# Attention with an additive bias: the second half of pair 0's q is loaded behind the first half of the bias

## The chip, the cores and the metric

The kernel runs on one core of a Trainium2 chip. The time is the device time of one execution in microseconds (us); the median of five executions stands for the kernel. The engines of the core are PE (matrix products), ACT (activation functions, here exponentials), DVE (vector work), POOL (GpSimd, which here issues most of the loads) and SP (which issues the stores and a few early loads). "Landing" is the moment at which a load's data is in on-chip memory and its semaphore is complete.

## The reference

Four batches of eight heads, 1024 positions, head size 64, all in float32; one bias matrix of 1024 by 1024 is shared by all heads.

```python
scores = scale * np.matmul(q, k.transpose(0, 1, 3, 2))      # scale = 1/8
scores = scores + bias
scores_max = np.max(scores, axis=-1, keepdims=True)
attn = np.exp(scores - scores_max) / (np.sum(np.exp(scores - scores_max), axis=-1, keepdims=True) + 1e-8)
return np.matmul(attn, v)
```

The kernel leaves the maximum out and uses exp(s + b) = exp(s) exp(b): the exponential of the bias is made once, and each head's exponentials are multiplied by it.

## The kernel before

**Tiling.** The 32 heads form 16 pairs. A pair's k and q are transposed on PE, so that the head's 64 dimensions of both heads fill the 128 rows. A *bank* is one product of 128 key positions with 512 query positions of one head: `banks` lists 512 of them, by pair, query half `qh`, key block `kc` and head. For pair 0, banks 0 to 15 have qh = 0, in the order of kc with the two heads beside each other, and banks 16 to 31 have qh = 1. A *slot* is one ACT instruction: slot 0 has bank 0, slot 1 has banks 1 and 2, and from slot 2 on each has three (slot 2: 3, 4, 5; slot 5: 12, 13, 14; slot 6: 15, 16, 17). S0, S1, ... are the slots here.

**The work of a slot.** `s_fill` has PE write the scores of a slot into one of two buffers (line 130). `s_exp` has ACT write the exponentials (line 137). `mul_pair` has DVE multiply them by the exponential of the bias (lines 156, 159, 162). `av_bank` has PE multiply them with v, which carries a column of ones for the denominators (line 187), and at the end of a head and half DVE divides (lines 197, 199) and SP stores.

**The bias.** It is loaded in two halves of 512 query rows, `btraw[:, :QC, :]` and `btraw[:, QC:, :]`, in 16 bits, 1 MB each. `b_fill(qh, k0)` transposes four key blocks of one half on PE into one of the same two score buffers (line 145), and `b_exp` takes the exponential (line 150). There are four such steps, called B(0,0), B(0,4), B(1,0) and B(1,4) here.

**The start.** Pair 0's first half of q and k comes by SP and ACT in float32 and is converted on the chip. The second half of k (`kr0`, line 261) and of q (`qr0`, line 262) and the first bias half (line 263) are issued by POOL one after the other on its one queue, and then v, the second bias half, and the loads of pairs 1 and 2. Slots 0 to 2 are written out by hand. Bank 8 is the first that reads the second half of k, bank 16 the first that reads the second half of q.

**The order of the rest.** From slot 3 on, a planner in the kernel's own text emits the instructions. It keeps three clocks (`t_act`, `t_pe`, `t_dve`), adds an assumed cost for each step, and takes in turn what can start first. What it emits is a fixed order for each engine: an instruction that waits holds back all behind it on its engine. The sequence of slots and bias steps is fixed by `order`: S3, S4, S5, S6, B(0,0), S7, B(0,4), S8, S9, B(1,0), S10, B(1,4), S11 and so on. Between these fills the planner puts the *pieces* (transpositions of half a k or half a q, `transpose_pe`, line 89, with the copy on DVE at line 98 for q and line 102 for k) and the products with v. A piece is placed no earlier than its data is assumed to land:

```python
bias_at = [13300, 20800]                                                 # line 338: the two bias halves, ns
raw_at = {0: (5900, 7800), 1: (22200, 23500), 2: (26000, 28500)}         # line 339: (k, q) of pairs 0, 1, 2
```

The times count in ns from the start of the span. These values steer the order alone; the waits themselves are made by semaphores, whatever the values are. The piece (0, 0, 1) is the second half of pair 0's q. When it has been copied, `run` issues the loads of pair 3 and of pair 2's v.

**The end.** The last eight banks of the last head (NB-8 to NB-1) are multiplied with v by `av_last` in two halves of 256 query rows (x = 0, 1), line 223. `pe_last` chooses which banks come next.

Of the kernel before, what the change touches and what calls it, by code (L numbers as in the profile page):

```python
# [15 lines left out]
def kernel(  # L16
# [15 lines left out]
    nc = tc.nc  # L32
# [7 lines left out]
    QC = NCH // 2  # L40
# [5 lines left out]
    bf_ = bias.rearrange("a b (p c) k -> p (a b c) k", p=P)  # L46
# [12 lines left out]
    btraw = consts.tile([P, NCH, S], BF)  # L59
# [47 lines left out]
    NB = len(banks)  # L107
# [106 lines left out]
    def av_last(x, bs, tag):  # L214
        first = len(last_left[x]) == 8
        if first:
            po[x] = (ps_x if tag != "s" else ps_s).tile([P, M, D1], F32, tag=tag, name="po")
        acc = po[x]
        for b in bs:
            last_left[x].remove(b)  # L220
        for i in range(M):
            for b in bs:
                nc.tensor.matmul(acc[:, i, :], e_at(b, 1)[:, 0, (x * M + i) * P:(x * M + i + 1) * P],
                                 vall[:, 2 * NP - 1, banks[b][3], :], start=first and i == 0 and b == bs[0],
                                 stop=not last_left[x] and b == bs[-1], skip_group_check=True)
        if last_left[x]:
            return None

        def evac():
            oh = small.tile([P, M, D], F32, name=f"oh{x}")  # L230
            rs = small.tile([P, M, 1], F32, name=f"rh{x}")
            nc.vector.reciprocal(rs[:], acc[:, :, D:D1])
            q = (nc.scalar, nc.sync)[x]
            if x == 0:
                for i in range(M):
                    nc.scalar.activation(oh[:, i, :], acc[:, i, :D], ACTF.Copy, scale=rs[:, i, :])
            else:
                nc.vector.tensor_tensor(oh[:], acc[:, :, :D], rs[:].to_broadcast([P, M, D]), op=ALU.mult)
            q.dma_start(out=of[2 * NP - 1][:, QC + x * M:QC + (x + 1) * M, :], in_=oh[:])
        return evac  # L240

    with tc.manual_schedule():
# [16 lines left out]
        nc.gpsimd.memset(qT0[D:, 0, :HQ], 0.0)  # L259
        nc.gpsimd.memset(qT0[:D, 1, :HQ], 0.0)  # L260
        nc.gpsimd.dma_start(out=kr0[:, :, QC:, :].rearrange("p t c d -> p t (c d)"), in_=kf[0][:, :, QC * D:])  # L261
        nc.gpsimd.dma_start(out=qr0[:, :, QC:, :].rearrange("p t c d -> p t (c d)"), in_=qf[0][:, :, QC * D:])
        nc.gpsimd.dma_start(out=btraw[:, :QC, :], in_=bf_[:, :QC, :])
        for x in range(2):
            for y in range(2):
                nc.vector.memset(mask[x * D:(x + 1) * D, y, :], 1.0 if x == y else 0.0)
# [68 lines left out]
        act_end = []  # L335
        x_free = {"xa": T0 - 500, "xb": T0 + 100}
        x_unit = {}
        bias_at = [13300, 20800]
        raw_at = {0: (5900, 7800), 1: (22200, 23500), 2: (26000, 28500)}
        pieces = [(0, 0, 1)]  # L340
        for pr in range(1, NP):
            pieces += [(pr, 1, 0), (pr, 0, 0), (pr, 1, 1), (pr, 0, 1)]
# [109 lines left out]
        def pe_last():  # L452

            best = None
            for x in range(2):
                left = last_left[x]
                if not left or (x == 1 and last_tag[0] is None):
                    continue
                steps = [[b] for b in left if b not in (NB - 4, NB - 3)] or [[NB - 4, NB - 3]]
                for bs in steps:  # L460
                    if any(b not in mul_at for b in bs):
                        continue
                    ready = max(mul_at[b] for b in bs) + SEM
                    tag = last_tag[x]
                    if tag is None and x == 0:
                        free, tag = min((x_free[y], y) for y in x_free)
                        ready = max(ready, free + SEM)
                    elif tag is None:
                        if len(act_end) < NO - 1 or len(filled) < NO:
                            continue  # L470
                        tag = "s"
                        ready = max(ready, act_end[NO - 2] + SEM)
                    c = (max(ready, t_pe), x, bs, tag)
                    if best is None or c[0] < best[0]:
                        best = c
            if best is None:
                return None
            ready, x, bs, tag = best
            cost = len(bs) * AV // 2

            def emit(t):
                if last_tag[x] is None and x == 0:
                    x_free[tag] = 1e12
                last_tag[x] = tag
                evac = av_last(x, bs, tag)
                if evac:
                    dve_q.append((t + cost + SEM, 1, EVAC, lambda t2: evac()))
            return ready, cost, emit

        def pe_av():  # L490
            if av_next >= NA:
                return pe_last()
            b = av_order[av_next]
            if b not in mul_at:
                return None
            ready = mul_at[b] + SEM
            u = unit_of(b)
            if banks[b][3] == 0:
                free, tag = min((x_free[x], x) for x in x_free)
                ready = max(ready, free + SEM)  # L500
            else:
                tag = x_unit[u]

            def emit(t):
                nonlocal av_next
                x_unit[u] = tag
                x_free[tag] = 1e12
                evac = av_bank(b, tag)
                av_next += 1
                if evac:  # L510
                    def run(t2):
                        evac()
                        x_free[tag] = t2 + EVAC
                    dve_q.append((t + AV + SEM, 3 if u == (NP - 1, 0, 1) else 1, EVAC, run))
            return ready, AV, emit
# [125 lines left out]
```

## Time and profile before

| what | value |
|---|---|
| median of 5 runs | 250.62 us (250.57 to 250.78) |
| the profiled execution | 250.62 us |
| its span, first to last instruction | 248.8 us |
| busy, share of the span | ACT 240.0 us (96%), PE 226.3 (91%), DVE 220.8 (89%), POOL 53.6 (22%) |
| ACT, exponentials of the scores, line 137 | 172 instructions, 230.1 us |
| ACT, exponentials of the bias, line 150 | 4 instructions, 7.5 us |
| PE, transpositions of the bias, line 145 | 64 matmuls, 4.7 us |
| chain that ended last, by engine | ACT 62%, PE 17%, DVE 12%, DMA 4% |

Busy times of one engine can overlap by about a tenth of a microsecond from one instruction to the next, so a sum of busy times is a little larger than the time it took. A row of the timeline gives the start, the length, the engine, the line, what is written and read, and how many instructions it joins; in square brackets stands the idle time before it and what ended it.

### The profile page before, as it was taken

Reading aid. Unit: us, or ns where it says so; the run is one execution under the profiler, and the core shown is the slowest. Engines: PE = TensorE matmul, PEld = TensorE weight load, DVE = VectorE, ACT = ScalarE, POOL = GpSimd, SP = SyncE. Lnnn points to the kernel's source line nnn. Section 1 sums busy time; section 2 is a strip of 40 time slices with the busy share of each in tenths; the row PEclk is TensorE's granted clock in tenths of the full one; section 3 lists DMA queues with packets and bytes.
Section 4 is the critical chain, followed back from the end, with each engine's and each line's share of the span. In section 5 each row is a group of like instructions: output and inputs, shape, how many; then the busy total and the mean of one; then the engine's idle time right before and its main releaser. Section 6 shows DMA issues by size and latency. Waiting matters only on the chain.

```text
span 248.8 us, 7157 instructions
## 1 busy us (share of the span) xinstructions
PE 226.3 (91%) x3105; PEld 140.9 (57%) x3160; DVE 220.8 (89%) x393; ACT 240.0 (96%) x183; POOL 53.6 (22%) x74
## 2 busy tenths in 40 slices
PE   7768999999999999999999999999999999998892
PEld 4245656566555665656656655555556555565561
DVE  5226999999999999999999999999999999999883
ACT  4999999999999999999999999999999999999992
POOL 6563534204013040315050500501600000000000
PEclk9999999999999999999999999999999999999999
DMA  5999999923924749495958951593891101020202
GB/s 122 181 202 191 199 118 212 93 84 48 165 49 85 86 89 126 87 129 78 137 75 105 138 67 44 79 137 42 116 102 42 45 16 72 3 84 3 87 25 63
DMA packets 48464, 23.80 MB, mean 96 GB/s; under 512 B 34480, under 2 KB 44592, under 8 KB 48176
## 3 DMA queue, kind: packets, MB, share of 16 engines
q0 software_dynamic: 42272, 14.42, 53.7%
q1 hardware_dynamic: 5872, 8.72, 9.7%
q8 instruction: 25, 0.41, 0.6%
q10 hardware_dynamic: 288, 0.20, 0.2%
q14 instruction: 7, 0.06, 0.1%
HBM read 29.36 MB, written 8.39 MB: 152 GB/s over the span
## 4 chain that ended last, share of the span: by engine, by line
ACT 62%; PE 17%; DVE 12%; DMA 4%; issue 2%; POOL 1%; ACTq 0%; POOLq 0%
ACT E L137 59%; PE ps L130 11%; DVE E L162 4%; PE po L187 4%; DMA btraw<-in_bias_dram 4%; ACT eb L150 3%; DVE qT L98 2%; DVE E L159 2%; PE px L89 2%; DVE oall L199 1%; DVE E L156 1%; DVE kT L102 1%; PE pb L145 0%; DVE rs L197 0%; POOL kr L261 0%
## 5 line engine op out<-in xcount | busy, mean ns | idle before, releaser
L137 ACT ACTIVATE E<-ps 128x1536 bf16<-128x1536 f32 (+2 forms) x172 | 230.1, 1700 | 0.7 <-PE ps L130 0.6
L130 PE MATMUL ps<-qT,kT 128*128 128x512 bf16 x457 | 134.5, 379 | 10.8 <-ACT E L137 5.2
L187 PEld LDWEIGHTS <-E 128*128 128x128 bf16 x2016 | 81.3, 98 | 40.1 <-DVE E L162 5.2
L187 PE MATMUL po<-vall,E 128*128 128x65 bf16 x2016 | 92.6, 194 | 3.3 <-DVE E L162 1.3
L159 DVE TENSOR_TENSOR E<-E,eb 128x2048 bf16<-128x2048 bf16 x66 | 79.8, 1217 | 6.6 <-ACT eb L150 6.2
L162 DVE TENSOR_TENSOR E<-E,eb 128x1024 bf16<-128x1024 bf16 x116 | 76.7, 684 | 2.7 <-ACT E L137 1.9
L130 PEld LDWEIGHTS <-kT 128*128 128x128 bf16 x512 | 45.3, 97 | 39.8 <-issue 8.4
L75 POOL DMA_DIRECT2D kr<-in_k_dram x15 | 10.5, 700 | 90.9 <-PE px L89 85.3
L81 POOL DMA_DIRECT2D vall<-in_v_dram x32 | 28.1, 883 | 5.2 <-DVE kT L315 4.3
L199 DVE TENSOR_TENSOR oall<-po,rs 128x256 f32<-128x256 f32 x63 | 26.7, 424 | 2.2
L98 DVE TENSOR_TENSOR qT<-px,mask 128x1024 bf16<-128x1024 bf16 x31 | 21.3, 688 | 3.9 <-PE px L89 3.1
L76 POOL DMA_DIRECT2D qr<-in_q_dram x15 | 10.8, 717 | 29.3 <-PE px L89 25.5
L102 DVE COPY kT<-px 128x512 bf16<-128x512 bf16 x30 | 12.6, 422 | 1.8 <-PE px L89 1.2
L197 DVE RECIPROCAL rs<-po 128x4 f32<-128x4 f32 x63 | 11.2, 178 | 2.0 <-PE po L187 1.7
L89 PE MATMUL px<-ident,qr 128*64 128x128 bf16 x248 | 12.8, 225 | 0.1
L89 PEld LDWEIGHTS <-qr 128*64 128x64 bf16 x248 | 8.0, 109 | 8.6 <-issue 6.3
L89 PE MATMUL px<-ident,kr 128*64 128x128 bf16 x240 | 12.4, 225 | 0.1
L89 PEld LDWEIGHTS <-kr 128*64 128x64 bf16 x240 | 7.7, 109 | 7.8 <-issue 3.2
L150 ACT ACTIVATE eb<-pb 128x2048 bf16<-128x2048 bf16 x4 | 7.5, 1877 | 0.1
L145 PE MATMUL pb<-ident,btraw 128*128 128x128 bf16 x64 | 4.7, 226 | 2.0 <-ACT eb L150 1.3
L145 PEld LDWEIGHTS <-btraw 128*128 128x128 bf16 x64 | 4.4, 147 | 2.9 <-issue 1.4
L156 DVE TENSOR_TENSOR E<-E,eb 128x1024 bf16<-128x1024 bf16 (+2 forms) x7 | 4.6, 686 | 0.2 <-ACT E L137 0.2
(44 smaller groups left out, 27.7 us busy)
## 6 DMA issues: line engine op xcount, KB each, us to landing
out_dram<-oall SPq DMA_DIRECT2D x28, 256.0 KB, 2.1
vall<-in_v_dram POOLq DMA_DIRECT2D x32, 128.0 KB, 6.1
kr<-in_k_dram POOLq DMA_DIRECT2D x15, 256.0 KB, 4.0
qr<-in_q_dram POOLq DMA_DIRECT2D x15, 256.0 KB, 5.3
btraw<-in_bias_dram POOLq DMA_DIRECT2D x2, 1024.0 KB, 9.7
out_dram<-oall SPq DMA_DIRECT2D x7, 128.0 KB, 3.9
k0f<-in_k_dram SPq DMA_DIRECT2D x2, 128.0 KB, 3.1
q0f<-in_q_dram ACTq DMA_DIRECT2D x1, 128.0 KB, 2.8
```

Of the source, the lines that this page charges most:

```text
L81: nc.gpsimd.dma_start(out=vall[:, 2 * pr + t, :, :D], in_=vf[pr, :, t])
L89: nc.tensor.transpose(px[t * D:(t + 1) * D, c, :], src[:, t, half * QC + c, :], ident[:])
L98: nc.vector.tensor_tensor(dst[:, :, half * HQ:(half + 1) * HQ], px.rearrange("p c q -> p (c q)").unsqueeze(1).to_broadcast([P, 2, HQ]), ma ...
L102: nc.vector.tensor_copy(dst[:, half * QC:(half + 1) * QC, :], px[:])
L130: nc.tensor.matmul(ps[:, j, :], kT[:, kc, :], qT[:, h, qh * HQ:(qh + 1) * HQ], start=True, stop=b not in late_bias)
L137: nc.scalar.activation(e_at(slots[g][0], n), open_ps.pop(("S", g))[:, :n, :], ACTF.Exp, scale=scale)
L150: nc.scalar.activation(eb[:, qh, k0:k0 + 4, :], open_ps.pop(("B", qh, k0))[:, :4, :], ACTF.Exp)
L159: nc.vector.tensor_tensor(e, e, eb[:, qh, kc:kc + 2, :].unsqueeze(2).to_broadcast([P, 2, 2, HQ]), op=ALU.mult)
L162: nc.vector.tensor_tensor(e, e, eb[:, qh, kc:kc + 1, :].to_broadcast([P, n, HQ]), op=ALU.mult)
L187: nc.tensor.matmul(acc[:, i, :], e[:, 0, i * P:(i + 1) * P], vall[:, 2 * pr + h, kc, :], start=(kc == 0 and i == 0), stop=(kc == NCH - 1), ...
L197: nc.vector.reciprocal(rs[:], acc[:, :, D:D1])
L199: nc.vector.tensor_tensor(oall[:, c0:c0 + QC, :], acc[:, :, :D], rs[:].to_broadcast([P, QC, D]), op=ALU.mult)
```

## The change

Three things differ. In the list of loads on POOL, the second half of pair 0's q goes behind the first half of the bias. The planner's assumed landings follow: the bias halves at 12.9 and 20.2 us, the second half of q at 13.7 us. In `pe_last`, banks NB-4 and NB-3 of the last head are no longer kept together as the last step, but are taken one by one like the others.

```diff
@@ the loads at the start
         nc.gpsimd.dma_start(out=kr0[:, :, QC:, :].rearrange("p t c d -> p t (c d)"), in_=kf[0][:, :, QC * D:])
+        nc.gpsimd.dma_start(out=btraw[:, :QC, :], in_=bf_[:, :QC, :])
         nc.gpsimd.dma_start(out=qr0[:, :, QC:, :].rearrange("p t c d -> p t (c d)"), in_=qf[0][:, :, QC * D:])
-        nc.gpsimd.dma_start(out=btraw[:, :QC, :], in_=bf_[:, :QC, :])
@@ the planner's landings
-        bias_at = [13300, 20800]
-        raw_at = {0: (5900, 7800), 1: (22200, 23500), 2: (26000, 28500)}
+        bias_at = [12900, 20200]
+        raw_at = {0: (5900, 13700), 1: (22200, 23500), 2: (26000, 28500)}
@@ pe_last
-                steps = [[b] for b in left if b not in (NB - 4, NB - 3)] or [[NB - 4, NB - 3]]
+                steps = [[b] for b in left]
```

## The prediction

> **What bounds the kernel now.** I read the page from its first part down, then the ACT timeline without its start, then PE and POOL over the first 25 us, then the chain. Part 1 puts ACT at 96% of the span, DVE and PE at 89% and 91%. The ACT timeline from 13 us on decides it:
>
> ```profile
> start us, us, engine line op out<-in xcount [idle before <-releaser]
> 13.39 1.49 ACT L137 ACTIVATE E<-ps 128x1536 bf16<-128x1536 f32 x1
> 14.97 1.88 ACT L150 ACTIVATE eb<-pb 128x2048 bf16<-128x2048 bf16 x1
> 16.74 1.45 ACT L137 ACTIVATE E<-ps 128x1536 bf16<-128x1536 f32 x1
> ...
> 27.51 215.95 ACT L137 ACTIVATE E<-ps 128x1536 bf16<-128x1536 f32 x161
> 244.31 0.52 ACT L236 ACTIVATE oh<-po,rh 128x64 f32<-128x64 f32 x2 [0.84 <-DVE rh L232]
> ```
>
> The last 161 exponentials stand in one unbroken row of 216 us. So whatever delays ACT before 27.5 us moves everything after it by as much, unless the end of the program absorbs it. The first row is pass S6 (slot 6 of `slots`, banks 15, 16 and 17); the second is the first exponential of the bias, B(0,0).
>
> The PE timeline shows what stood around S6, and where PE waits for memory:
>
> ```profile
> 10.29 0.41 PE L89 MATMUL px<-ident,qr 128*64 128x128 bf16 x8
> 10.90 0.81 PE L130 MATMUL ps<-qT,kT 128*128 128x512 bf16 x3 [0.19 <-ACT E L137]
> 12.24 0.81 PE L130 MATMUL ps<-qT,kT 128*128 128x512 bf16 x3 [0.54 <-ACT E L137]
> 13.74 1.19 PE L145 MATMUL pb<-ident,btraw 128*128 128x128 bf16 x16 [0.69 <-DMA btraw<-in_bias_dram]
> ```
>
> Row one is the transposition of the second half of pair 0's q; rows two and three are the fills of S5 and S6; row four is the fill of B(0,0), the only one that waits for a load. S6's exponential starts at 13.39 and the next pass at 14.97, 1.58 later. Elsewhere a pass costs 1.34 (16.84 to 18.19 in the chain). The bias thus costs ACT 1.58 - 1.34 = 0.24 now. That is all that an earlier bias can give back at this place.
>
> The issues on POOL, and from the answers for lines 261, 262 and 263 the times to landing (3.6, 5.2, 9.7):
>
> ```profile
> 2.42 0.83 POOL L261 DMA_DIRECT2D kr<-in_k_dram  x1
> 3.25 0.73 POOL L262 DMA_DIRECT2D qr<-in_q_dram  x1
> 3.96 0.60 POOL L263 DMA_DIRECT2D btraw<-in_bias_dram  x1
> 8.81 1.75 POOL L81 DMA_DIRECT2D vall<-in_v_dram  x2 [4.26 <-DVE kT L315]
> ```
>
> So k's half lands at 6.02, q's half at 8.45, the bias half at 13.70 (2.42 + 3.6, 3.25 + 5.2, 3.96 + 9.74).
>
> **What the Trainium skill says.** "DMA: Bandwidth & Descriptors", section "Two DMAs through the same engine are not ordered": within one queue of one DMA engine, descriptors start in order. The trace agrees: the three landings follow the issues, with the wide one last. So when two of them exchange places on the one queue, the place of their common end stays. "Perfetto Trace Analysis", section "DMA Instruction — SWDGE (GPSIMD)": the bar of such a DMA ends when its descriptors are written, not with the data. Here the bias bar is 0.60 and the landing 9.74, so the bars say nothing of the swap of landings. "TensorE: Matmul & The Clock Gate", "Part 1: The HAM clock gate": PE runs at half clock after an idle window of about 3.4 us; no run so far shows it after the start. "Architectural detail" on the same page: PE's queue can pull weight loads ahead of matmuls in flight, and nothing more is said to overtake. The trace agrees in that no fill stands ahead of B(0,0)'s wait.
>
> **The change, part by part.**
>
> *The two loads.* They keep their bars (0.73 and 0.60), and the instructions on POOL behind them keep their times, since the next (v) waits for line 315 until 8.81. The queue still carries k, q and bias, in the order k, bias, q. The work in front of the last of the three is the same as before, so a first value for q's landing is 13.70, the old landing of the last. Bounds: the bias can come earlier by no less than the moved issue (0.73) and no more than the step from k's to q's landing (8.45 - 6.02 = 2.43), so it lands between 11.3 and 13.0. Behind it q takes at least 0.66 (128 KB at the bias's own rate, 1024 KB in 13.70 - 8.45 = 5.25) and at most the 2.43 that it took before. Sum: 11.9 to 15.4. Part of the 2.43 was shared with the head of the bias, which no longer stands beside it, so I take 13.5, a little under the conserved 13.70.
>
> *The order of PE.* The listing of the built program shows the transposition of q's second half moved from ahead of S5 to just ahead of S6, which cannot lie later: banks 16 and 17 are the first with qh = 1. B(0,0) still stands behind S6, because the fixed order S3, S4, S5, S6, B(0,0) is not touched. So the early bias finds PE waiting for q. S5 keeps its time, 10.90, as the row above says that it waits for ACT.
>
> *The wait that is added.* From q's landing to S6's exponential, with durations from the rows: 0.05 to the first transposition (13.69 to 13.74 at the bias's landing), 0.41 for the eight, 0.05 to DVE (10.70 to 10.75), 0.69 for the copy with the mask (line 98), 0.05 back to PE (8.77 to 8.82 after line 315), 0.59 for the two matmuls that need it (bank 15 reads the first half and runs ahead), 0.03 to ACT. Sum 1.87. With q at 13.50, S6's exponential starts at 15.37 in place of 13.39: ACT stands idle for 1.98. Behind the waiting transposition PE holds S6, B(0,0), S7 and the rest; DVE holds the mask copy, and behind it the first product, which waits for B(0,0) anyway. POOL waits for none of it: pair 3's loads need the transposed buffer, and the third of q goes out only at 20.79.
>
> *What follows it.* B(0,0) is filled behind S6 on PE: its 1.19 run from about 15.3 to 16.5, under S6's exponential, which ends at 15.37 + 1.34 = 16.71. This hides it with 0.2 to spare, and the old 0.24 of the bias goes. B(0,0) starts at 16.71 against 14.97, so 1.74 later. DVE's first product (16.88 before) waits for it and shifts alike, so DVE and PE keep their distance to ACT. Pair 1's k and q, which were 22.6 and 24.0 on PE, find their data no later than before.
>
> *The second bias half* is due at 20.2 rather than 20.8 in the emission model. Its load is issued behind the same three; its fill waited for ACT, not for memory (at 24.55 and 21.40 the rows name ACT, DVE or nothing). Taken at 0.
>
> *The new order of the rest.* The emission model takes other times, so from S9 on the pieces and the products of attention and v fall in other places for most of the run. The listing has 2016 such matmuls and 512 scores as before, and three fewer groups on DVE. With ACT unbroken from 27.51 to 243.46 there is almost nothing to win: 0.1 visible idle time on L150. A replanned order can lose where a fill comes late. Bounds -0.3 to +0.6; taken at 0.
>
> *The end.* The last banks NB-4 and NB-3 may now go one by one, in place of as a pair at the end. It moves 2 matmuls of the 32 of line 223 (x32, 1.5 us, so 0.05 each). The chain there runs over DVE's last products and evacuation (241.67 to 244.16), not over these. Taken at 0, bounds -0.15 and +0.15.
>
> *Sum:* +1.74 on a profiled execution of 250.62 (span 248.8 and 1.8 around it), which is also the median: 252.4.
>
> **The rivals.**
>
> (a) *q lands early and the wait is mostly hidden.* The 2.43 of q would have been contention with the bias, and the bias lands near 11.3. For it: half of the old q took place beside the bias. Against it: 1 MB still stands in front. At q = 11.9, S6 starts at 13.77, 0.38 late less 0.24: 250.8. Nearly no change; q at 12.5 gives 251.4.
>
> (b) *Faster.* If q lands before 11.52 (13.39 - 1.87), S6 is on time, and B(0,0) comes 0.24 sooner, as the bias is no longer what it waits for: 250.4. It decides from the point where bias and q are both through by 11.5, below my lower bound, so it needs loads that run faster than any here. Only with the whole 0.3 that the new order could win would this be measurable, at 250.1.
>
> (c) *PE goes cold in the hole.* PE would be idle from 11.71 to 13.55, 1.8 us, against the window of 3.4 which the page states. No gap of this size stands in the trace after the start. If it happens, the cold rows at the start give the price: a fill of three took 1.32 at 5.47 rather than 0.81, so +0.4 for two matmuls and their transpositions, and B(0,0) then takes about 1.9 and misses its cover by 0.5: 252.4 + 0.9 = 253.3. The same time comes out of a q at 14.4.
>
> (d) *The arrival values do nothing.* The loads don't change places because the queue interleaves them. Then PE's moved transposition costs nothing, as S5 waits for ACT either way, and the time is 250.6. The wide bias behind q now lands 5.25 after it, which speaks against it.
>
> **How the numbers follow.** Main case, ACT waits 1.3 to 2.5 us for q: 0.70, at 252.4, own range 251.7 to 253.0. Late or cold (c): 0.13, 253.0 to 254.2. Mostly hidden (a): 0.11, 250.8 to 251.7. (b) 0.03, (d) 0.03. The measurement can tell some 0.2% (0.5 us) from no change. Below 250.1: the end of (b), 0.02. Within 0.5: the rest of (b), (d) and the part of (a) below 251.1, together 0.07. The rest, 0.91, is slower. The range 251.1 to 253.4 leaves out the ends of (c), and (b), (d) and the lower end of (a).
>
> **What would show it.** In the changed profile, the transposition on line 89 for qr waits for a DMA of q with more than 1 us idle, ACT's S6 waits for line 130 by about 2 us, B(0,0) follows S6 without a gap, and the ACT row from there to the end is unbroken and 1.7 later. The prediction is wrong if q lands before 12, if ACT shows new gaps after 30 us that add up to more than 0.6, or if the end after the last exponential is longer.

## The result, and the profile after

The changed kernel takes 252.28 us in the middle of 43 runs, the kernel before 250.88 in the middle of 80 (the larger number of runs moves it from the 250.62 of the first five). The ratio is 1.0067, with a 95% interval of 1.0053 to 1.0082. By the middle values the change is 1.4 us slower, by the ratio 1.7. (A ratio leaves out executions more than 1.5% above the fastest of their kernel, which drops five of the 22 of experiment 9, four of the 22 of experiment 11 and one of the 14 of experiment 8 below; the middle values keep them.)

The times of the changed kernel stand in two groups. Of 44 executions with a recorded clock 25 lie under 252.9, with a median of 251.80, and 22 of these have a mean granted PE clock of 0.994 or more. The other 19 have a median of 253.91, and all of them a clock of 0.993 or less. This clock is a mean over the whole execution and is also lowered by the idle stretch at the very end (0.71 from 245 to 249 us in the first profile), so it marks the groups only roughly. The first profile is of the lower group: 251.17, span 249.4. Its span is only 0.6 longer than the one before, because its first exponential of scores started at 5.58 rather than 6.12; from there to B(0,0) it lost 1.07 (15.50 - 5.58 against 14.97 - 6.12).

The chain of waits of the changed kernel, from its account of the first 30 us (start, length, what):

```profile
3.81 8.47 DMA qr<-in_q_dram
12.28 0.04 issue
12.32 0.43 PE px L89 x8
12.75 0.02 issue
12.78 0.70 DVE qT L98
13.48 0.04 issue
13.52 0.61 PE ps L130 x2
14.13 0.02 issue
14.15 1.45 ACT E L137
15.60 1.77 ACT eb L150
```

In the chain before, the bias stood in this place:

```profile
3.96 9.74 DMA btraw<-in_bias_dram
```

Now q stands there. It lands at 12.28, and S6's exponential starts 1.87 later, through one transposition, one copy and two products. The PE and the ACT timeline show both sides of the hole:

```profile
10.34 0.81 PE L130 MATMUL ps<-qT,kT 128*128 128x512 bf16 x3 [0.75 <-ACT E L137]
12.32 0.41 PE L89 MATMUL px<-ident,qr 128*64 128x128 bf16 x8 [1.17 <-DMA qr<-in_q_dram]
13.52 0.59 PE L130 MATMUL ps<-qT,kT 128*128 128x512 bf16 x2 [0.47 <-DVE qT L98]
13.95 1.13 PE L145 MATMUL pb<-ident,btraw 128*128 128x128 bf16 x16
```

```profile
7.50 5.48 ACT L137 ACTIVATE E<-ps 128x1536 bf16<-128x1536 f32 x4 [0.21 <-PE ps L130]
14.15 1.45 ACT L137 ACTIVATE E<-ps 128x1536 bf16<-128x1536 f32 x1 [1.18 <-PE ps L130]
15.50 1.87 ACT L150 ACTIVATE eb<-pb 128x2048 bf16<-128x2048 bf16 x1
...
29.34 214.63 ACT L137 ACTIVATE E<-ps 128x1536 bf16<-128x1536 f32 x160
```

The bias landed 8.3 after its issue at 3.25, at 11.55. B(0,0) no longer waits for memory but stands behind S6. ACT loses 1.18 ahead of S6 and nothing visible after it: the long row is unbroken again. (The row is shown from a view that begins at 30 us. Whole, it has 161 exponentials and starts at 28.01, against 27.51 before.) At the end, the last products with v on line 223 start at 243.11 (242.60 before) and the last two copies on ACT at 244.77 (244.31). The end moved with the rest.

### The profile page after: what moved, and what is told of

The parts are those of the page before. It is cut to its first block, busy times and chain, and to the rows that moved or that the text cites. A ratio compares the mean times of both kernels' runs of the same rounds, so it can differ in the third digit from the quotient of the medians.

```text
span 249.4 us, 7160 instructions
## 1 busy us (share of the span) xinstructions
PE 225.3 (90%) x3106; PEld 140.8 (56%) x3160; DVE 220.8 (89%) x393; ACT 240.0 (96%) x183; POOL 53.6 (21%) x74
## 3 DMA queue, kind: packets, MB, share of 16 engines
q0 software_dynamic: 42272, 14.42, 53.6%
## 4 chain that ended last, share of the span: by engine, by line
ACT 70%; PE 17%; DVE 6%; DMA 3%; issue 2%; POOL 1%; ACTq 0%; POOLq 0%
ACT E L137 67%; PE ps L130 10%; PE po L187 4%; DMA qr<-in_q_dram 3%; ACT eb L150 3%; PE px L89 2%; DVE E L162 2%; DVE E L156 1%; DVE qT L98 1%; DVE oall L199 1%; DVE E L159 0%; POOL kr L261 0%; POOL btraw L262 0%; POOL qT L259 0%; POOL qT L260 0%
## 5 line engine op out<-in xcount | busy, mean ns | idle before, releaser
L187 PE MATMUL po<-vall,E 128*128 128x65 bf16 x2016 | 94.5, 194 | 3.0 <-DVE E L162 1.2
L75 POOL DMA_DIRECT2D kr<-in_k_dram x15 | 10.5, 703 | 93.6 <-PE px L89 84.4
```

The source lines that it names most:

```text
L187: nc.tensor.matmul(acc[:, i, :], e[:, 0, i * P:(i + 1) * P], vall[:, 2 * pr + h, kc, :], start=(kc == 0 and i == 0), stop=(kc == NCH - 1), ...
```

## The experiments

Each kernel was timed beside the kernel before on the same chip. Theory A is the hole: S6 follows q's landing, and the PE clock may fall in it. Theory B has q's landing vary and nothing else. Theory C puts the loss on the planner's new order. "Lower" and "upper" are the two groups of the changed kernel, below and above 252.9.

**1. The changed kernel again.**

> The changed kernel once more, unaltered, for its spread and a second profile. Theory A (a hole on PE ahead of S6 costs ACT about 1.2 us, and in part of the executions the PE clock falls in that hole and costs about 2 us more): times fall into two groups, near 251.8 and near 254, and the upper group has the lower granted clock. Theory B (q simply lands up to 2 us later in some executions): a spread of times without two groups, and the clock of a late execution no lower than the idle time explains. Theory C (the new order of the planner costs the time): one group, near 252.3.

253.18 in the middle of 12 (251.09 to 254.47), ratio 1.0083 (1.005 to 1.0115). The two groups are there again: five from 251.09 to 252.35, all with a clock of 0.995 or more, seven from 252.99 with 0.992 or less. Its profile is of the lower group: PE's transposition starts at 12.60, S6 at 14.42.

**2. The hole filled with products of zeros on PE.**

```diff
+        hot = ps_x.tile([P, HQ // 2], F32, tag="xb" if tag == "xa" else "xa", name="hot")
+        for i in range(10):                      # ahead of the 8 transpositions of piece (0, 0, 1)
+            nc.tensor.matmul(hot[:], zeros[:, :P], zeros[:], start=True, stop=True)
...
+        for i in range(4):                       # behind them
+            nc.tensor.matmul(hot[:], zeros[:, :P], zeros[:], start=True, stop=True)
```

> The changed kernel with 14 products of zeros on PE beside the waiting transposition: 10 ahead of it, while q is on its way, and 4 behind it, while DVE copies. They fill the hole and delay nothing that is ready. Theory A: the upper group of times is gone or much smaller, all near 251.8 (1.2 us above the kernel before at most). Theory B: the same two-sided spread as the changed kernel, since loads are not touched. Theory C: no difference from the changed kernel.

252.12 in the middle of 12 (250.3 to 253.9), ratio 1.0042 (1.0007 to 1.0078). The executions spread as before, but the upper ones come down: four from 252.61 to 252.89 and only two above (253.67 and 253.9, the two with the lowest clocks, 0.990 and 0.989). Its profile is one of the four, and it fits both A and B. The PE timeline (the added products are on line 90 of its text, the transposition on 94):

```profile
10.89 1.25 PE L90 MATMUL hot<-zeros 128*128 128x256 bf16 x10
14.16 0.41 PE L94 MATMUL px<-ident,qr 128*64 128x128 bf16 x8 [2.02 <-DMA qr<-in_q_dram]
14.50 0.61 PE L97 MATMUL hot<-zeros 128*128 128x256 bf16 x4
```

q landed at 14.1, 1.8 later than in the first profile, in a kernel whose loads are the same. So landings do vary that much (B). The eight transpositions took 0.41, at full clock, and S6 followed 1.83 after their start (15.99). The added products also cut the time without a product from 3.1 (11.05 to 14.16) to 2.02. That they kept the clock up is likely, but this is one trace of twelve executions. Four of the twelve (250.3 to 250.81) are faster than the fastest of the changed kernel (250.98), which no theory said and no trace explains.

**3. The bias step ahead of S6.**

```diff
-        for at, x in ((4, (0, 0)), (6, (0, 4)), (9, (1, 0)), (11, (1, 4))):
+        for at, x in ((3, (0, 0)), (6, (0, 4)), (9, (1, 0)), (11, (1, 4))):
```

> The changed kernel with the first bias step B(0,0) put ahead of S6 in the fixed order, so that the bias, which now lands first (11.55 in the profile), is filled while q is still on its way. Theory A: ACT goes from S5 to B(0,0) without a gap, S6 follows 1.77 later, when q has been copied (14.15 in the profile against about 14.7), and the 0.24 that the bias cost before is saved: 250.4 to 250.7. Theory B: the same, as a late q is covered up to about 12.9. Theory C: still near 252.3, since the order of the rest is again another one than before.

252.45 in the middle of 8 (251.37 to 252.89), ratio 1.0058 (1.0033 to 1.0083). A and B missed; C's number fits, but not by C's reason. In the profile the bias landed at 13.75 (10.5 after its issue) in place of 11.55, so PE waited for it in q's place:

```profile
13.78 1.22 PE L145 MATMUL pb<-ident,btraw 128*128 128x128 bf16 x16 [2.22 <-DMA btraw<-in_bias_dram]
14.93 0.64 PE L89 MATMUL px<-ident,qr 128*64 128x128 bf16 x8
16.36 2.15 PE L130 MATMUL ps<-qT,kT 128*128 128x512 bf16 x5 [0.25 <-DVE qT L98]
```

Here the cold PE (one at the lowered clock) is seen: eight transpositions take 0.64 rather than 0.41. The sixteen of the bias, right behind the idle 2.22, had still taken 1.22, against 1.19 before; the clock fell only at 14.8. To be second on the queue does not make a load early in every execution. Why its best execution is still at 251.37, one trace of a late one can't tell; that stays open.

**4. The new order with the loads in their old places.**

```diff
+        nc.gpsimd.dma_start(out=qr0[:, :, QC:, :].rearrange("p t c d -> p t (c d)"), in_=qf[0][:, :, QC * D:])
         nc.gpsimd.dma_start(out=btraw[:, :QC, :], in_=bf_[:, :QC, :])
-        nc.gpsimd.dma_start(out=qr0[:, :, QC:, :].rearrange("p t c d -> p t (c d)"), in_=qf[0][:, :, QC * D:])
```

> The loads in their old order, with the changed kernel's whole order of instructions (new landings in the planner, new end). Theory A: q lands at about 8.4 as before, PE does not wait for it, S6 waits at most for the mask copy, and the bias lands last as before: 250.5 to 250.9, no change within 0.2%. Theory B: likewise no change. Theory C: the loss remains, near 252.3.

251.94 in the middle of 16 (250.81 to 253.75), ratio 1.0057 (1.0033 to 1.008). Theory A said no change: a clear miss. The PE timeline of this kernel shows a second wait that the change brings:

```profile
19.52 0.81 PE L130 MATMUL ps<-qT,kT 128*128 128x512 bf16 x3 [0.29 <-ACT eb L150]
21.09 0.41 PE L89 MATMUL px<-ident,kr 128*64 128x128 bf16 x8 [0.76 <-DMA kr<-in_k_dram]
21.43 0.29 PE L187 MATMUL po<-vall,E 128*128 128x65 bf16 x4
21.57 1.16 PE L145 MATMUL pb<-ident,btraw 128*128 128x128 bf16 x16
```

The planner, which assumes a q at 13.7, now puts the first transposition of pair 1's k ahead of B(1,0); before, it stood behind it. PE waits there for pair 1's k, and B(1,0) and ACT wait behind it:

```profile
22.77 1.88 ACT L150 ACTIVATE eb<-pb 128x2048 bf16<-128x2048 bf16 x1 [0.61 <-PE pb L145]
```

This profile (250.98) is the second fastest of the sixteen, so it shows where the new order waits, but not how long it waits in the slower executions. Six of these have 252.54 to 253.75 with a clock of 0.993 or less, without q behind the bias; no trace of one was taken.

**5. The exchange of the loads in the kernel before, with its old order.** The same two lines exchanged in the kernel before, and nothing else.

> The kernel before with the two loads exchanged and nothing else; the planner still believes q at 7.8 and puts its transposition ahead of S5. Theory A (the hole is set by q's landing): S5 is now held too. With q at 12.3, S5 starts at about 13.6 in place of 12.1, S6 at 14.95 and B(0,0) at 16.3, 0.8 later than in the changed kernel: 252.8 to 253.4 in the middle. Theory C (the planner's new order is what costs, as the order alone gave +1.06): near 250.9.

254.1 in the middle of 6 (252.55 to 255.05), against 250.61: ratio 1.013 (1.009 to 1.0169). S5 is held as well, as A said, and more was lost than A said. In the windows of this kernel (length, then busy time of PE, PEld, DVE, ACT and POOL with the number of instructions, the granted clock, the share of the DMA engines and GB/s) the clock is at one half while q is waited for:

```profile
8.00:12.00 4.00, 0.85 (x3) 0.19 (x2) 0.00 (x0) 3.61 (x3) 4.00 (x6) 0.84 1.05 183
12.00:16.00 4.00, 1.73 (x11) 0.83 (x12) 0.69 (x1) 0.00 (x0) 2.58 (x4) 0.50 1.64 198
```

ACT stood idle for 4.72 ahead of S5. So the planner's new landings do what they are meant to: alone the exchange costs 3.5 by the middle values, with them 1.4.

**6. The order alone, with pair 1's k put back behind B(1,0).** Experiment 4 with one entry of the planner changed (pair 1's k by 1.4 us, its q by 0.1):

```diff
-        raw_at = {0: (5900, 13700), 1: (22200, 23500), 2: (26000, 28500)}
+        raw_at = {0: (5900, 13700), 1: (23600, 23600), 2: (26000, 28500)}
```

> The loads in their old order and the changed kernel's order of instructions, but with the landing of pair 1's k and q set to 23.6 in the planner (22.2 and 23.5 before), so that the first transposition of pair 1's k goes behind B(1,0) again, as it stood in the kernel before. Theory C1 (the order alone loses because that transposition waits for its load ahead of the third bias step: 0.76 on PE and 0.61 on ACT in its profile): the loss is gone, 250.5 to 251.1. Theory C2 (it loses by the rest of the new order, or by S5 standing ahead of q): near 251.9 as before.

250.91 in the middle of 14 against 250.61, ratio 1.0013 (0.9995 to 1.0031). C1 holds: with this transposition back behind B(1,0) the loss of experiment 4 is gone, and with it the slow executions (the slowest is 252.09). The rest of the new order, S5 ahead of q and the new end among it, costs nothing that can be measured; the interval leaves room for at most 0.3%.

**7. q made later.**

```diff
         nc.gpsimd.dma_start(out=btraw[:, :QC, :], in_=bf_[:, :QC, :])
+        spare = consts.tile([P, 2, QC, D], BF, name="spare")
+        nc.gpsimd.dma_start(out=spare.rearrange("p t c d -> p t (c d)"), in_=kf[0][:, :, :QC * D])
```

> The changed kernel with one more load of 128 KB (pair 0's first half of k once more, into a buffer that nobody reads) between the bias and q on POOL's queue; nothing waits for it. It moves q's landing by about 0.7 to 1.5. Theory A: S6 follows q by 1.87 wherever it lands, so the times move up by as much, and more executions fall into the upper group with the lower clock: middle 253.2 to 254.4. If q's landing does not set S6: no change from 252.3.

254.77 in the middle of 6 (252.11 to 255.29), ratio 1.014 (1.0095 to 1.0186), above the 253.2 to 254.4 that A expected. All six have a clock of 0.989 to 0.991, also the two at 252.11 and 252.44. In the profile PE waits 3.66 for q, starts at 14.85, and S6 follows at 17.23, 2.38 after it; the extra half microsecond is the clock (a granted clock of 0.87 from 12 to 16 us and 0.70 from 16 to 20).

**8. q on SP's queue in the kernel before.** The load on POOL is dropped; SP loads the same half in float32 behind k's, into a tile `q1f`.

```diff
+        nc.sync.dma_start(out=q1f.rearrange("p t c d -> p t (c d)"), in_=qf[0][:, :, QC * D:])
...
+        nc.vector.tensor_copy(qr0[:, :, QC:, :], q1f[:])      # behind the copy of k's second half
```

> The kernel before with the second half of pair 0's q taken off POOL's queue: SP loads it in float32 behind k's first half, and DVE converts it in a time in which it is idle. The bias then stands second on POOL's queue, as in the changed kernel, and nothing stands behind it. Theory A: the bias lands at about 11.5 to 13.7, q before 10, B(0,0) waits for ACT alone, and the executions in which the bias came late before (the upper part of the kernel before, 252 and more) come down: middle 250.0 to 250.5, upper end under 251.5. If the landings are not what spreads the kernel before: the same spread as it, 250.9 in the middle.

250.99 in the middle of 14 (249.82 to 254.54), ratio 1.0019 (0.9992 to 1.0045): not faster, and A missed. The bias wait is gone (B(0,0)'s fill on PE waits for ACT), but the second half of k landed 4.7 after its issue, at 7.1, against 6.0 before, and ACT stood 1.10 idle ahead of S2. Whether the load on SP did that is not settled, as k's half took 4.5 in experiment 1 too. What made its two slowest executions, the trace does not show.

**9. The changed kernel with pair 1's k later.** The value of experiment 6, in the changed kernel.

> The changed kernel with the same one value altered as in the run with the order alone: pair 1's loads set to 23.6, so that the first transposition of pair 1's k goes behind B(1,0). Theory A (in the changed kernel q's hole comes first and covers the other wait: B(1,0) reaches ACT at q's landing + 10.85, against the landing of pair 1's k + 1.75, which is q's landing + 10.05): nothing is won, 251.9 to 252.7 in the middle. Theory D (the two losses add, each about half): about 251.3 to 251.6, some 0.8 less than the changed kernel.

253.05 in the middle of 22 (250.22 to 254.29), against 251.05: ratio 1.0048 (1.0024 to 1.0073), without the five slowest. The middle lies above what either theory said. With all 22 the mean is 252.69, against 251.04 for the kernel before in the same series; in the first result the two means were 252.73 and 251.05. So nothing that can be measured is won, as A said. The profiles agree: here B(0,0) and B(1,0) stand at 15.59 and 23.25 on ACT, 7.66 apart, and in the changed kernel at 15.50 and 23.13, 7.63 apart, both without a gap. In the upper-group profile of experiment 12 they are 7.66 apart (17.85 and 25.51), again without one.

**10. The loads of the start ahead of POOL's memsets, in the kernel before.**

```diff
-        nc.gpsimd.memset(qT0[D:, 0, :HQ], 0.0)
-        nc.gpsimd.memset(qT0[:D, 1, :HQ], 0.0)
         nc.gpsimd.dma_start(out=kr0[:, :, QC:, :] ...
...
+        nc.gpsimd.memset(qT0[D:, 0, :HQ], 0.0)                # now behind the three loads
+        nc.gpsimd.memset(qT0[:D, 1, :HQ], 0.0)
```

> The kernel before with the three loads of the start issued on POOL ahead of the two memsets of pair 0's q tile (1.1 us of POOL) in place of behind them. All three landings come about 1.1 earlier. Theory A: the bias no longer sets B(0,0) (0.24 in the profile, up to 1.5 in late executions), ACT alone does: 250.0 to 250.4 in the middle, and the upper end comes down. If the landings are not what spreads the kernel before: 250.6 to 250.9 as it is.

250.36 in the middle of 22 (249.28 to 252.43), against 251.05 for the kernel before: ratio 0.9979 (0.9961 to 0.9998). This version is faster than the kernel before by about 0.2%, by an interval that just leaves out no change, and so faster than both kernels. The middle is as A said; the upper end did not come down (252.43, against 252.33 before). In its profile B(0,0) no longer waits for memory:

```profile
13.32 1.15 PE L145 MATMUL pb<-ident,btraw 128*128 128x128 bf16 x16 [0.54 <-ACT E L137]
```

**11. The same step in the changed kernel.**

> The changed kernel with the same step: loads ahead of the memsets. q lands about 1.1 earlier, near 11.2 to 13. Theory A: S6 follows by 1.87, so the loss shrinks by about as much: 250.6 to 251.6 in the middle, and fewer executions in the upper group. If q's landing is not the cause: 252.3.

252.03 in the middle of 22 (250.39 to 254.81), ratio 1.0036 (1.0016 to 1.0057), without the four slowest. By the middle values it stands 0.98 above the kernel before, where the change stands 1.40 above it. With all 22 the mean is 1.47 above, where the change has 1.68, and seven of the 22 lie above 252.9 (19 of 44 for the change). So at most a part of the loss is gone, and the runs do not show clearly that any is. The expected 250.6 to 251.6 was not reached, and the PE timeline shows one reason:

```profile
11.92 0.41 PE L89 MATMUL px<-ident,qr 128*64 128x128 bf16 x8 [0.21 <-DMA qr<-in_q_dram]
...
21.80 0.41 PE L89 MATMUL px<-ident,kr 128*64 128x128 bf16 x8 [0.86 <-DMA kr<-in_k_dram]
```

q's transposition starts 0.40 earlier than in the changed kernel's first profile. The hole closes by more, to 0.21, because S5's fill ends 0.56 later: the second of SP's two loads of k landed 4.5 after its issue rather than 2.9, and the first exponential started at 6.57 rather than 5.58. With the hole closed, the other wait of experiment 4 takes its place and costs ACT 0.73 ahead of B(1,0). Pair 1's loads were not issued earlier (v, ahead of them, waits for line 315 as before), so they are not moved by this step.

**12. The changed kernel, traced once more.**

> One more look at the changed kernel, unaltered, for the trace of an execution of its upper group, if it falls there (about 2 in 5 do). Theory A then shows: q's landing near 14, PE idle for over 2 us ahead of its transposition, a granted clock of about 0.5 to 0.9 in the slices after it, transpositions of 0.54 to 0.64 in place of 0.41 for eight, and S6 later by 2 to 3 than in the first profile. Theory B (loads alone): q near 14, but full clock and 0.41. In an execution of the lower group: q near 12.3, full clock, S6 at 14.2.

253.62, an execution of the upper group, with the clock at 0.988; what it shows is what A expected. The PE timeline, and below it two of its windows:

```profile
13.98 0.64 PE L89 MATMUL px<-ident,qr 128*64 128x128 bf16 x8 [2.29 <-DMA qr<-in_q_dram]
15.41 1.01 PE L130 MATMUL ps<-qT,kT 128*128 128x512 bf16 x2 [0.25 <-DVE qT L98]
16.21 1.60 PE L145 MATMUL pb<-ident,btraw 128*128 128x128 bf16 x16
```

```profile
12.00:16.00 4.00, 1.77 (x11) 0.79 (x12) 0.69 (x1) 1.51 (x2) 3.58 (x5) 0.73 1.62 194
16.00:20.00 4.00, 2.84 (x24) 2.03 (x23) 0.24 (x1) 3.55 (x3) 0.71 (x1) 0.84 1.02 201
```

And ACT, with S6 and B(0,0):

```profile
16.45 1.45 ACT L137 ACTIVATE E<-ps 128x1536 bf16<-128x1536 f32 x1 [2.94 <-PE ps L130]
17.85 1.88 ACT L150 ACTIVATE eb<-pb 128x2048 bf16<-128x2048 bf16 x1
```

Against the lower group's profile, q is 1.66 later (13.98 against 12.32), and from there to S6 it takes 2.47 in place of 1.83. The two terms give S6's 2.30 (16.45 - 14.15), and the whole execution is 2.45 longer (253.62 - 251.17). So this execution of the upper group is a late q (1.66) and a PE that has gone cold (0.64). That the other eighteen are alike is inferred from their times and clocks; they were not traced.

Profiles that have q last on the queue and B(0,0) behind S6, side by side (us; the time is that of the profiled execution; in experiment 2 the idle time counts from the last product of zeros):

| kernel (experiment) | PE idle before q's transposition | transposition starts | S6 starts | between | time | time less S6's start |
|---|---|---|---|---|---|---|
| changed, with the loads first (11) | 0.21 | 11.92 | 13.75 | 1.83 | 251.99 | 238.24 |
| changed | 1.17 | 12.32 | 14.15 | 1.83 | 251.17 | 237.02 |
| changed, k later (9) | 0.72 | 12.41 | 14.24 | 1.83 | 251.26 | 237.02 |
| changed, again (1) | 0.73 | 12.60 | 14.42 | 1.82 | 251.85 | 237.43 |
| changed, hole filled (2) | 2.02 | 14.16 | 15.99 | 1.83 | 252.61 | 236.62 |
| changed, upper group (12) | 2.29 | 13.98 | 16.45 | 2.47 | 253.62 | 237.17 |
| changed, q late (7) | 3.66 | 14.85 | 17.23 | 2.38 | 254.52 | 237.29 |

From S6 to the end it takes 236.6 to 237.4, wherever S6 stands. The one exception is experiment 11, with its second wait. The kernel before had 250.62 - 13.39 = 237.23. (Experiment 3 has another order, and in experiment 5 S5 waits as well.)

## Why the prediction was right, and where it was not

The time was forecast at 252.4 and is 252.28, and the mechanism that was forecast, S6 waiting for q on PE, is the one that the traces show. That the number came so close is in good part luck. The forecast added 1.74 to the 250.62 of the first five runs; by the middle values the change cost 1.40, on top of 250.88. And 252.28 lies between two groups of executions, at 251.80 and 253.91, which the forecast's one landing of q did not have. Point by point:

- **The added wait** (sum of 1.87 from q's landing to S6). Right: 1.87 in the first profile.
- **The order of PE**, S5 not touched, B(0,0) behind S6 and no gain from the early bias. Right: S5 ran on in the ACT row, and B(0,0) followed S6 1.35 later.
- **What follows**: no new gap later and the end moved alike. Right, in the profiles of both groups.
- **The two loads**: the step took one landing of q, 13.50, from the old landing of the last of the three. That was wrong as a step. q lands at 12.28 in one execution and 13.94 in another of the same kernel, and the 13.70 of the bias was itself one case (3.96 + 9.2 = 13.2 in experiment 4). The range of 11.9 to 15.4 held both. What varies is the bias in front (11.55 and 13.25, past the upper bound of 13.0); q itself came 0.7 behind it each time, close to the 0.66 that the prediction had as the least. The lower group's profile therefore loses less than the forecast (1.18 of ACT in place of 1.98) and the upper group's more (2.94).
- **Rival (c), PE cold in the hole**, at 0.13. Too low: 19 of 44 executions lie in or above its range of 253.0 to 254.2, and the one that was traced is such a case, with a late q besides. Its price was +0.9; measured are 0.64 up to S6, and 0.05 more up to B(0,0), whose fill took 1.60 and not 1.9. It was set aside because a hole of 1.8 us was held against the idle window of about 3.4 us of the Trainium skill, "TensorE: Matmul & The Clock Gate", "Part 1: The HAM clock gate". The measurement decides: the clock had fallen by the end of 2.29 idle (experiment 12). The same section calls the window free-running, which the prediction left out, and the last section has the falls that a gap's length alone does not explain. The rows at the start from which the price was taken have a granted clock of 1.00 in the trace, so that they were cold is not shown.
- **The new order of the rest**, "Taken at 0", bounds -0.3 to +0.6. This step failed, hidden behind the main one. Alone, it costs 1.06 by the middle values (experiment 4), and "Pair 1's k and q, which were 22.6 and 24.0 on PE, find their data no later than before" holds only while q's hole holds everything back. Pair 1's k was moved ahead of B(1,0), and no row was read for when its load lands. Together the two losses do not add: the wait that ends later sets B(1,0), q's in the three profiles of the changed kernel, that for pair 1's k in experiment 11.
- **The second bias half and the end**, both at 0. The profiles show nothing against it. Neither was tried alone, but experiment 6 has both and is not measurably slower (1.0013).
- **Rivals (a), (b) and (d)** did not come about. (a) is closest in the kernel with the loads first, and there another wait took over.

## What to carry to other kernels

A load that is exchanged with a larger one on the same queue wins nothing if the order of the engine that uses both still asks for the small one first: look at which of the two is consumed first, not at which is larger. Turning that order round (experiment 3) did not win anything here either, as the bias came late there. Assumed arrival times in a planner move more than the piece that they name, so list everything that now stands ahead of its own data, each with the landing read from the trace. And where the landings of one kernel differ by 2 us from one execution to the next, forecast the two or three cases and their shares, for one profile shows one of them.

## What the runs showed of the hardware that was not expected

- **The landing of one and the same sequence of loads varies.** In the nine profiles with q behind the bias on POOL's queue, the 1 MB bias half took 8.3 to 8.9 us from its issue in four (the changed kernel, 1, 9, 11) and 10.0 to 10.5 in five (2, 3, 5, 7, 12). q landed 0.6 to 0.8 behind it, 1.4 with the added load of experiment 7. What makes a landing late, no run shows.
- **The length of the idle time did not by itself decide when PE's clock fell.** Read from short windows of the traces, the granted clock went from 1.00 to 0.50 1.2 us after PE's last product in experiment 5 (at 10.75, and the hole went on to 14.27), 2.2 us after it in experiment 12 (at 13.9), and 3.8 us after it in experiment 7 (at 15.0, when PE had just begun again). In experiment 3 it fell at 14.8, a microsecond after a hole of 2.22 was over. It stayed at 1.00 through the hole of 1.17 of the first profile and that of 2.02 in experiment 2.
- **The half clock came in pieces of 3.4 us**: 3.4 us in experiments 3, 7 and 12, twice as long (6.8) in experiment 5. In the 3.4 us ahead of each fall PE had been busy for 0.15 to 1.5 us. How little work lets the clock fall, the runs do not separate.
- **A cold clock costs little by itself here**: 0.64 between q's transposition and S6 in experiment 12, of the 2.45 that separate the two groups' profiles.
